# Loading the last quarter row of six tiles in two parts, in a row-wise maximum that skips NaN

## The chip, the cores and the metric

The kernel runs on one core of one Trainium2 chip. The metric is device time in microseconds (us) of one execution; lower is better.

## The reference

```python
def setup_inputs():
    batch, seq, dim = 32, 2048, 2048
    x = np.random.randn(batch, seq, dim).astype(np.float32)
    mask = np.random.rand(batch, seq, dim) < 0.1
    x[mask] = np.nan
    return {"x": x, "axis": -1}

def reference(x, axis):
    return np.nanmax(x, axis=axis).astype(np.float32)
```

For each of 65536 rows of 2048 floats it takes the largest value that isn't NaN. That is 537 MB to read and 0.26 MB to write.

## The kernel before

The rows are split into groups, and within a group each of the 128 partitions holds a run of whole rows that lie behind each other in memory. The work goes through tiles. A tile is one entry of `TILES`: a triple of loads, cleaning pieces and reductions, each counted in quarter rows of 512 floats (`Q`), that is 2 KB in each partition. The first tile has 4 quarter rows, nearly all others have 28, seven whole rows in every partition (7168 KB in all); the tiles of the last stage have 28 too, but are loaded in two to nine parts. Three buffers `xt` take the tiles in turn.

A tile goes through four steps, on four queues:

- **SP** issues its loads at line 309 (SP is the sync engine's queue, and the sixteen DMA engines carry the loads out). A load waits until DVE has done the last reduction of the tile that held the buffer before (`free`), and until the load that used the same semaphore before has landed (`lanes`; there are 14 semaphores, taken in turn). SP works strictly in order.
- **ACT** reads the upper 16 bits of each float and makes an ordered key of them in a buffer `kt` (line 227); a key piece waits for the loads that overlap its columns.
- **POOL** writes keys back to the upper halves in `xt` in such a way that NaN becomes very small (line 237); some pieces go to ACT instead.
- **DVE** takes the maximum over each row into `acc` (line 244).

In a usual tile the pieces are 7, 9 and 12 quarter rows and the reductions 16 and 12. The class `Order` (`add`, line 220) keeps the order by semaphores: each engine has one that counts its instructions, each load semaphore counts 16 a load, and an instruction waits only for what its engine has not already seen. At the end, six stores bring the maxima out.

What the change touches is the loop over a tile's loads:

```python
                for c in loads:
                    c *= Q
                    a, b = at, at + c
                    e = order.add("sp", nc.sync,
                        lambda: nc.sync.dma_start(
                            out=xt[:, a:b], in_=xg[:, base + a : base + b]),
                        before + lanes[turn], lane=f"load{turn}", step=16)
```

Of the kernel before, what the change touches and what calls it, by code (L numbers as in the profile page):

```python
# [10 lines left out]
Q = D // 4  # L11
# [43 lines left out]

APART = (70, 71, 72, 73)
WIDE = 7
BUFS = 3

KEYS = 3 * D  # L60
# [18 lines left out]
def total(pieces):  # L79
    return sum(sum(map(abs, p)) if isinstance(p, tuple) else abs(p) for p in pieces)  # L80
# [93 lines left out]
def kernel(  # L174
# [16 lines left out]
    P = nc.NUM_PARTITIONS  # L191
# [21 lines left out]
    top, warm = scalars[:, 0:1], scalars[:, 1:2]  # L213
    xts = [sing.tile([P, WIDE * D], i32, name=f"xt{i}") for i in range(BUFS)]
    kts = [sing.tile([P, KEYS], u16, name=f"kt{i}") for i in range(NKEYS)]
# [4 lines left out]
    with tc.tile_critical():  # L220
# [51 lines left out]

        free = [[] for _ in range(BUFS)]
        kfree = [[] for _ in range(NKEYS)]
# [8 lines left out]
        number = 0  # L283
# [6 lines left out]
        for gi, (s, g) in enumerate(zip(rows, GROUPS)):  # L290
            xg = xr[r0 : r0 + P * s].rearrange("(p s) d -> p (s d)", p=P)
# [4 lines left out]
            base = 0  # L296
            for loads, pieces, reds in g:
                assert sum(loads) == total(pieces) == sum(reds)
                xt, before = xts[number % BUFS], free[number % BUFS]
                number += 1  # L300
                landed = []
                at = 0
                for c in loads:
                    c *= Q
                    a, b = at, at + c
                    e = order.add(
                        "sp",
                        nc.sync,
                        lambda: nc.sync.dma_start(  # L309
                            out=xt[:, a:b], in_=xg[:, base + a : base + b]  # L310
                        ),
                        before + lanes[turn],
                        lane=f"load{turn}",
                        step=16,
                    )
                    lanes[turn] = [e]
                    turn = (turn + 1) % LANES
                    landed.append((a, b, e))
                    at += c
                clean = []  # L320
                after = []
                at = done = 0
# [41 lines left out]
                for parts in pieces:  # L364
                    parts = parts if isinstance(parts, tuple) else (parts,)
                    c = int(sum(map(abs, parts))) * Q
                    here = [l for a, b, l in landed if a < at + c and b > at]
                    kold = []
                    if used + c > KEYS:
# [9 lines left out]
                        out=kts[key][:, used : used + c],  # L379
                        in_=xt[:, at : at + c].bitcast(i16)[:, 1::2],  # L380
# [6 lines left out]
                    for c in parts:  # L387
                        back, wait, c = c < 0, isinstance(c, float), int(abs(c)) * Q
# [8 lines left out]
                        else:  # L397
# [3 lines left out]
                                out=to,  # L401
# [9 lines left out]
                        while reds and done + reds[0] <= min([at] + open_):  # L411
# [8 lines left out]
                            else:  # L420
# [5 lines left out]
                                out=to,  # L426
                                in_=xt[:, lo:done]
# [6 lines left out]
                            after.append(e)  # L434
                free[(number - 1) % BUFS] = after[-1:]
                base += at
# [65 lines left out]
```

## Time and profile before

| | before |
|---|---|
| time, median of 2 runs | 1251.94 us (1251.53 to 1252.36) |
| time of the profiled execution | 1251.85 us |
| its span in the profile | 1250.1 us |
| busy: POOL, DVE, ACT | 1168.7, 1110.8, 965.5 us |
| DMA, mean over the span | 430 GB/s |

The span runs from the first to the last instruction of the program; the 1.75 us beside it lie around it. In the profile an engine's busy time leaves out its waits. A DMA engine moves packets; here a packet is what a load brings to one partition, and a small packet of 4 bytes behind a load's last one raises the load's semaphore by one. The load has landed when the semaphore has come to 16 more. Line 309 names the issue of a load, 227 the keys, 237 POOL's pieces and 244 the reductions.

### The profile page before, as it was taken

The page shows a single profiled execution, that of the slowest core. Times are in us where ns is not written, and L with a number is a line of the kernel's source. Part 1 is how long each engine was busy: PE and PEld are TensorE (multiplying, and loading weights), DVE is VectorE, ACT ScalarE, POOL GpSimd, SP SyncE. Part 2 cuts the span into 40 slices and gives each one's busy share as a digit, 9 for nine tenths or more (in the row PEclk, how much of TensorE's full clock was granted, in tenths as well). Part 3 has the DMA queues.
Part 4 walks back from the last instruction along what each step waited for, and adds up shares of the span by engine and source line. Part 5 has one row for each costly group of instructions (what it writes and reads, how often), then busy time and mean ns, then how long its engine had stood idle before and what let it go on. Part 6 is the DMA issues. An engine that isn't in the chain of part 4 may idle for free.

```text
span 1250.1 us, 886 instructions
## 1 busy us (share of the span) xinstructions
DVE 1110.8 (89%) x181; ACT 965.5 (77%) x273; POOL 1168.7 (93%) x242
## 2 busy tenths in 40 slices
DVE  0788989888889888898988888988888999999999
ACT  3777887778777877788777877777777778999998
POOL 2999989998999899998999899999999999989998
DMA  9999999999999999999999999999999999999997
GB/s 415 435 417 440 440 440 429 422 441 440 435 420 437 440 437 433 422 440 440 437 429 426 440 440 433 422 437 440 437 433 422 441 437 423 438 431 429 428 428 311
DMA packets 15991, 537.20 MB, mean 430 GB/s; under 512 B 2544, under 2 KB 2544, under 8 KB 3568
## 3 DMA queue, kind: packets, MB, share of 16 engines
q1 hardware_dynamic: 15984, 537.14, 99.4%
q14 instruction: 7, 0.06, 0.0%
HBM read 536.87 MB, written 0.26 MB: 430 GB/s over the span
## 4 chain that ended last, share of the span: by engine, by line
DMA 40%; DVE 29%; POOL 22%; ACT 9%; issue 1%; SPq 0%
DMA xt<-in_x_dram 40%; DVE acc L244 29%; POOL xt L237 22%; ACT kt L227 8%; ACT xt L227 1%; SPq L309 0%; DVE none L250 0%; DVE acc L264 0%; SPq L465 0%; SPq L220 0%
## 5 line engine op out<-in xcount | busy, mean ns | idle before, releaser
L237 POOL TENSOR_SCALAR xt<-kt 128x3584 int16<-128x3584 uint16 (+11 forms) x236 | 1167.6, 4948 | 77.6 <-ACT kt L227 63.5
L244 DVE TENSOR_REDUCE acc<-xt 128x3 f32<-128x6144 f32 (+4 forms) x175 | 1107.5, 6379 | 136.6 <-POOL xt L237 129.2
L227 ACT ACTIVATE kt<-xt 128x3584 uint16<-128x3584 int16 (+9 forms) x247 | 913.4, 3734 | 278.3 <-DMA xt<-in_x_dram 258.1
L227 ACT ACTIVATE xt<-kt 128x512 int16<-128x512 uint16 (+6 forms) x24 | 52.9, 2203 | 0.7
L227 ACT ACT_TABLE_LOAD x1 | 1.3, 1283 | 0.9 <-SPq L220 0.9
L244 DVE TENSOR_REDUCE xt<-xt 128x1 f32<-128x1536 f32 x1 | 1.7, 1742 | 0.0
L270 DVE MEMSET scalars<- 128x1 f32 x1 | 0.1, 59 | 1.0 <-SPq L220 1.0
L250 DVE TENSOR_SCALAR none<-acc 128x414 int32<-128x414 f32 (+1 forms) x2 | 0.8, 380 | 0.1
L264 DVE TENSOR_TENSOR acc<-acc,none 128x414 int32<-128x414 int32 (+1 forms) x2 | 0.7, 374 | 0.1
L250 POOL TENSOR_SCALAR late<-acc 128x91 int32<-128x91 f32 x1 | 0.5, 547 | 0.1
L264 POOL TENSOR_TENSOR acc<-acc,late 128x91 int32<-128x91 int32 x1 | 0.3, 341 | 0.1
L483 POOL MEMSET const-float32-0.0<- 128x1 f32 x1 | 0.1, 99 | 0.2 <-issue 0.2
L227 ACT ACTIVATE scalars<-scalars 128x1 f32<-128x1 f32 x1 | 0.2, 203 | 0.0
L483 POOL MEMSET const-bfloat16-1.0<- 128x1 bf16 x1 | 0.1, 102 | 0.0
L483 POOL MEMSET const-uint8-127<- 128x1 uint8 x1 | 0.1, 102 | 0.0
L483 POOL MEMSET const-float32-1.0<- 128x1 f32 x1 | 0.1, 99 | 0.0
## 6 DMA issues: line engine op xcount, KB each, us to landing
xt<-in_x_dram SPq DMA_DIRECT2D x61, 7168.0 KB, 22.6
xt<-in_x_dram SPq DMA_DIRECT2D x2, 5120.0 KB, 17.5
xt<-in_x_dram SPq DMA_DIRECT2D x3, 2816.0 KB, 22.7
xt<-in_x_dram SPq DMA_DIRECT2D x4, 2048.0 KB, 22.3
xt<-in_x_dram SPq DMA_DIRECT2D x5, 1536.0 KB, 29.1
xt<-in_x_dram SPq DMA_DIRECT2D x2, 3584.0 KB, 24.7
xt<-in_x_dram SPq DMA_DIRECT2D x6, 1024.0 KB, 26.8
xt<-in_x_dram SPq DMA_DIRECT2D x3, 1792.0 KB, 30.0
```

The costliest lines, as they stand in the source:

```text
L227: lambda: nc.scalar.activation(**kw),
L237: lambda: nc.gpsimd.tensor_scalar(**kw),
L244: return order.add("dve", nc.vector, lambda: do(**kw), deps)
L250: lambda: engine.tensor_scalar(out=none, in0=acc, scalar1=NONE, scalar2=float(0x00800000), op0=ALU.is_equal, op1=ALU.mult,),
L264: lambda: engine.tensor_tensor(out=bits, in0=bits, in1=none, op=op),
L270: e_top = order.add("dve", nc.vector, lambda: nc.vector.memset(top, EDGE), [])
L483: nc = _bacc.Bacc("TRN2", target_bir_lowering=False, num_devices=1)
```

## The change

In the tiles with `number` 4 to 9 (`number` counts from 1) the single load of 28 quarter rows becomes three: 27 quarter rows of all 128 partitions, then the last quarter row of the first 120, 126, 117, 108, 121 or 100 partitions, then the last quarter row of the other 8, 2, 11, 20, 7 or 28. SP issues them in this order. Each has a semaphore of its own from the 14. `landed` gets the column range of each, and so the key pieces that overlap the last quarter row wait for three loads.

```diff
+CUTS = {4: 120, 5: 126, 6: 117, 7: 108, 8: 121, 9: 100}
...
-                for c in loads:
-                    c *= Q
-                    a, b = at, at + c
+                cut = CUTS.get(number)
+                runs = [(sum(loads[: i + 1]) * Q, 0, P) for i in range(len(loads))]
+                if cut:
+                    (end, _, _), *rest = runs
+                    runs = [(end - Q, 0, P), (end, 0, cut), (end, cut, P), *rest]
+                for b, p, q in runs:
+                    a = at
                     e = order.add(
                         "sp",
                         nc.sync,
                         lambda: nc.sync.dma_start(
-                            out=xt[:, a:b], in_=xg[:, base + a : base + b]
+                            out=xt[p:q, a:b], in_=xg[p:q, base + a : base + b]
                         ),
...
-                    at += c
+                    if q == P:
+                        at = b
```

Nothing else is changed: the other tiles' loads, the key pieces, the cleaning and the reductions stand as before. The loads become 12 more.

## The prediction

> **What bounds the kernel now.** First the page's rows on the DMA engines, with the row of the loads' sizes:
>
> ```profile
> DMA  9999999999999999999999999999999999999997
> q1 hardware_dynamic: 15984, 537.14, 99.4%
> xt<-in_x_dram SPq DMA_DIRECT2D x61, 7168.0 KB, 22.6
> ```
>
> The 16 DMA engines are busy for 99.4% of the span, in every slice but the last. Then the windows by stage, for the long middle (columns: stretch, its length, busy time of DVE, ACT and POOL, clock, DMA share, GB/s):
>
> ```profile
> 210.00:850.00 640.00, 572.42 (x77) 488.40 (x118) 609.93 (x111) 1.00 1.00 434
> ```
>
> POOL works 609.93 of 640 us, which is near, but the DMA share is 1.00. Next the waits, of the engines and of SP's queue:
>
> ```profile
> ACT kt L227 <- DMA xt<-in_x_dram: 258.1, 69, 15.0
> ```
>
> ```profile
> SPq L309 <- DVE acc L244: 1155.7, 71, 37.8
> ```
>
> ACT, the first engine to touch a tile, waits for a landing at nearly every tile. SP waits for DVE to give a buffer back, which looks as if DVE set the pace. The chain in order of time says whether it does:
>
> ```profile
> 67.83 22.62 DMA xt<-in_x_dram
> 90.45 0.02 issue
> 90.47 3.20 ACT kt L227
> ...
> 103.38 15.16 DVE acc L244 x2
> 118.54 0.02 issue
> 118.56 22.67 DMA xt<-in_x_dram
> ```
>
> DVE frees the buffer at 67.8 and the load that it releases lands at 90.45; the load before it landed at 73.58 (last increment of its semaphore). So the load is issued 5.8 us before the transfer ahead of it ends, and queues. The chain's "DMA 40%" is mostly queueing, and the pace is the transfer itself: 16.9 us a tile. DVE and POOL have those 5.8 us to spare.
>
> The records of single packets say how fast a DMA engine is. A 57344-byte packet (one partition's 28 quarter rows) takes 2116 ns and the next starts 3 ns before it ends, 2113 ns a step; eight such packets and a 4-byte one of 6 ns make 16.91 us, the pace above. From the 10th to the 90th percentile the 2116 ns doesn't move, so no engine is slower than another. A packet of 2048 bytes, in the kernel's only 256 KB load, takes 84 ns, a step of 81. The two steps differ by 2032 ns over 54 KiB, 37.6 ns a KiB, which leaves some 6 ns for the packet itself; a packet of 55296 bytes is therefore 75.3 ns shorter than one of 57344.
>
> The sixteen increments of a load's semaphore say how the engines stand to each other. The first tile's come within 0.56 us, those at 560 us within 0.92, the last loads' within 1.3 to 1.4. The steps between fall at 246, 255, 386, 940, 999 and 1130 us, where the trace has 8 KB instruction packets (309 ns each) on one engine or another. At the end the engines stand, in us behind the last: 1.29, 1.25, 1.24, 1.24, 1.18, 1.17, 1.17, 1.07, 0.99, 0.90, 0.83, 0.80, 0.74, 0.40, 0.15, 0. The mean is 0.9. **The time is set by the DMA engine that ends last**, and all that better balance could give is these 0.9 us.
>
> **The change, part by part.** (1) In six tiles the 57344-byte packets become 55296: every engine has 48 of them, so it saves 48 x 75.3 ns = 3.61 us. (2) The 128 packets of 2 KB that this takes out come back in two loads a tile, 768 packets of 81 ns in all. Equally spread that is 48 an engine, 3.89 us. (3) Each of the 12 added loads ends with a 4-byte packet on each engine that it uses, at most 12 x 6 ns = 0.07 us. With an equal spread the sum is 3.89 - 3.61 + 0.07 = **+0.35 us**, the lower bound.
>
> (4) The spread can't be equal. The trace shows loads of 128 partitions alone, and in each every engine gets eight packets. No row shows 120 or 8 partitions. Bounds: the equal spread, +0.35 us, and all packets of a split load on one engine, 768 x 0.081 - 3.61 = +58.6 us. I take the case nearest to what is seen, equal shares for those engines that a load uses, on as many engines as divide its partitions, and the same ones left out each time: 15, 14, 13, 12, 11 and 10 engines for the large parts, with 8, 9, 9, 9, 11 and 10 packets each; 8, 2, 11, 10, 7 and 14 engines for the rests, with 1, 1, 1, 2, 1 and 2. Against 48, the sixteen engines then have +16, +16, five times +15, +14, +13, +13, +1, -11, -20, -29, -40 and -48 packets (they sum to 0). Each of the ten loaded engines ends later by 61 to 64 x 0.081 - 3.61 + about 0.07 = +1.4 to +1.64 us; the last is relieved by 3.61. Which of them are the late ones now the trace doesn't tell. If the last one is loaded (10 in 16), the end moves by +1.4 to +1.64. If it is relieved, the next counts: -0.15 + 1.6 = +1.45 at most; and if the five latest were all among the relieved, the others still make -0.8 + 1.4 = +0.6. Over all such orders I take **+1.4 us**. That an engine ends 3.6 us early buys nothing, since ACT needs all shares of a tile.
>
> [...]
>
> (5) SP issues 12 more loads of 0.33 to 0.43 us (the first three issues are 0.43 apart). SP is idle 1155.7 us, and the large part is issued first, as early as now; the small ones follow 0.8 us later, 22 us before they land. Cost nothing; without that cover 12 x 0.43 = 5.2 us. Behind them on SP stands the next tile's load, 16.9 us later. (6) The 14 load semaphores are taken in turn, so 12 more loads only rotate them; a load waits for the one 14 loads earlier, five tiles back in tiles 4 to 9. Nothing. (7) ACT's last key piece of these tiles now also waits for the two small loads. They land within some 1.5 us after the large part, and ACT comes to this piece 7.5 us after its first (39.73 and 47.23 in the timeline); behind it on ACT stands the next tile's first piece, which waits for its own load. Nothing; if a part came 10 us late, POOL's and DVE's 5.8 us would be used up first. (8) In the tail the engines follow the landings: ACT still waits 2.9 us for loads from 1195 us on, in six waits, so a later landing moves the end in full.
>
> The profiled execution took 1251.85 us (span 1250.1), 0.1 below the median of 1251.94. Sum: 1251.85 + 1.4 = **1253.3 us**, to a tenth; its own range is 1252.3 to 1254.
>
> **The rivals.** *Almost equal spread*: shares differ by at most one packet, and the loaded engines alternate. +0.35 us and a little, 1252.2. For it: 128 partitions spread evenly in every DMA; against: it needs unequal shares within a load, which none shows. *Two engines meet*: a partition of the split loads is written by another engine than in the loads of 128, and if neighbours then share a way into memory, packets take twice their time. Bound: all 64 small packets of an engine doubled, 64 x 0.081 = 5.2 us more, 1258.5; half of them, 1255.9. For it: the engines run at one unvarying rate, as if each had a way of its own; against: no row, since the trace has loads of 128 partitions alone. [...] *A gain*: the rows happen to be taken from the late engines alone. At best the mean of 0.9 less 0.35, -0.55 us, 1251.3; against it stand the +61 packets on ten engines. *Slower, by crowding*: the number of engines has to be a power of two that divides the partitions; 128 on 16 doesn't exclude it. Then 120, 126, 117, 108, 121 and 100 run on 8, 2, 1, 4, 1 and 4 engines, the rests on 8, 2, 1, 4, 1 and 4, and the first engine gets 368 + 32 = 400 packets: 400 x 0.081 - 3.61 + 0.07 = +28.9 us, 1280.8. It would be slower by over 2% (25 us) from 353 packets on one engine. No row speaks for it, and none excludes it. *No effect*: the extra is lost in the spread of runs, 1251.9.
>
> **How the numbers follow.** Forecast 0.65, almost equal 0.14, engines meeting 0.12, a gain 0.04, crowding 0.03, no effect 0.02. The range takes in the forecast, the almost equal spread and the meeting up to somewhat over its half: 1251.7 to 1256.5. About what a measurement of this kernel can tell from no change is 2%, 25 us: only crowding is slower by more than that, with a little for costs I don't see, 0.04; a gain of 25 us has no place in engines that are never idle, 0.01; within 2%, 0.95.
>
> **What would show it.** In the profile after: 12 more issues at the load's line, packets of 55296 bytes for tiles 4 to 9 and 768 more of 2048 bytes, 84 ns each (168 if engines meet). The increments of a small load's semaphore should be bunched by engines used, and the spread between first and last increment should grow from 0.5 us to 4 to 6 us between tiles 4 and 10, and stay there. The last load should land near 1244.0 instead of 1242.6. POOL, DVE and ACT keep their busy times to 1 us. I'd be wrong if a pause appears in the DMA rows after tile 4, if the spread stays near 1.3 us, if the tiles' pace leaves 16.9 us after tile 9, or if the end moves by more than 5 us.

## The result, and the profile after

The changed kernel takes 1259.61 us (1259.36 and 1259.86) against 1251.94: a ratio of 1.0063, 95% interval 1.0047 to 1.0079. In five later executions three gave 1256.89, 1260.71 and 1261.66 us, against 1251.97 (1.0055, 1.0035 to 1.0075). The comparisons leave out executions over 1.5% above a kernel's fastest; the other two of these five, at 1392 and 1445 us, are such, and the experiments show that the change itself makes them. The forecast was 1253.3 us, with a range up to 1256.5: its sign was right, its size too small.

The page after, rows on the DMA engines and the loads:

```profile
GB/s 413 433 414 378 418 436 425 425 438 438 432 436 434 432 434 428 438 438 434 436 432 432 438 427 436 438 438 432 432 434 436 428 431 431 430 431 432 430 427 309
DMA packets 16886, 537.20 MB, mean 427 GB/s; under 512 B 2671, under 2 KB 2671, under 8 KB 4463
q1 hardware_dynamic: 16879, 537.14, 99.4%
...
xt<-in_x_dram SPq DMA_DIRECT2D x55, 7168.0 KB, 22.6
xt<-in_x_dram SPq DMA_DIRECT2D x6, 6912.0 KB, 26.0
```

The engines are as busy as before, 99.4%, in a longer span (1258.1 us): they don't wait more, they take longer for the same bytes. The fourth slice of 31.5 us has 378 GB/s. The windows narrow it down:

```profile
40.00:107.00 67.00, 59.31 (x9) 49.42 (x12) 65.05 (x13) 1.00 1.00 423
107.00:130.00 23.00, 20.53 (x3) 12.90 (x4) 20.53 (x4) 1.00 1.03 357
...
150.00:850.00 700.00, 624.39 (x84) 535.95 (x131) 662.36 (x119) 1.00 1.00 434
```

The same stretch in the kernel before:

```profile
107.00:130.00 23.00, 21.22 (x4) 18.11 (x5) 22.44 (x5) 1.00 0.99 429
```

From 150 us on it is the 434 GB/s of before. While tile 8 is loaded it is 357, where the kernel before has 429. Waits and chain say the same from the other side:

```profile
ACT kt L229 <- DMA xt<-in_x_dram: 265.4, 70, 15.0
```

```profile
136.68 29.17 DMA xt<-in_x_dram
165.85 0.02 issue
165.87 3.20 ACT kt L229
...
193.95 22.56 DMA xt<-in_x_dram
```

ACT waits 7.3 us more for landings. The load issued at 136.68 (tile 10's) takes 29.17 us, one issued at 193.95 again 22.56. Busy times of the engines stay: DVE 1110.9, ACT 965.9, POOL 1169.0.

The last increments of each tile's loads, in us after those of before, and what each tile adds, beside what the prediction's shares give for the busiest engine (8 to 11 packets and the rest's, times 0.081, less 0.60):

| tile, first part | late by | added | by shares |
|---|---|---|---|
| 4, 120 | 0.45 | 0.56 | 0.14 |
| 5, 126 | 0.95 | 0.50 | 0.22 |
| 6, 117 | 1.64 | 0.69 | 0.22 |
| 7, 108 | 2.46 | 0.82 | 0.30 |
| 8, 121 | 6.81 | 4.35 | 0.38 |
| 9, 100 | 7.84 | 1.03 | 0.38 |
| 10, whole | 7.75 | -0.09 | 0 |

(Tiles 1 to 3, before any cut, stand at -0.11.)

The packet records show two things. First, where the small packets stand, at the joint between one tile's load and the next, many of them are stretched (451 of 768 take over 90 ns, the longest 187 and not 84), and so are the large ones beside them: most take 250 to 720 ns more than their usual 2041 or 2116, the longest 988. Second, behind tile 7's joint the stretch doesn't end: seven large packets of every engine, 112 in all, take 2454 to 2464 ns. This is a *slow step*: the time from one packet to the next is 1.206 times the usual, on all engines alike. It ends when tile 8's own small packets come. Seven packets of +0.42 us are 2.9 us.

### The profile page after: what moved, and what is told of

Its sections match the earlier page's. It is cut to its first block, busy times and chain, and to the rows that moved or that the text cites. A ratio compares the mean times of both kernels' runs of the same rounds, so it can differ in the third digit from the quotient of the medians.

```text
span 1258.1 us, 904 instructions
## 1 busy us (share of the span) xinstructions
DVE 1110.9 (88%) x181; ACT 965.9 (77%) x273; POOL 1169.0 (93%) x242
## 2 busy tenths in 40 slices
DMA packets 16886, 537.20 MB, mean 427 GB/s; under 512 B 2671, under 2 KB 2671, under 8 KB 4463
## 3 DMA queue, kind: packets, MB, share of 16 engines
q1 hardware_dynamic: 16879, 537.14, 99.4%
## 4 chain that ended last, share of the span: by engine, by line
DMA 38%; DVE 31%; POOL 22%; ACT 8%; issue 1%; SPq 0%
DMA xt<-in_x_dram 38%; DVE acc L246 31%; POOL xt L239 22%; ACT kt L229 7%; ACT xt L229 1%; SPq L315 0%; DVE none L252 0%; DVE acc L266 0%; SPq L472 0%; SPq L222 0%
```

## The experiments

Two theories on the loss beside the small packets: *crossing*, a partition of a part load is written by another engine than usual, and two engines meet on one way to it; and *shares*, engines with unequal work, or packets and loads as such. On the slow step: it follows from how the engines' traffic stands to each other, or it belongs to tile 8's own cut and addresses. All kernels change one line or two; where nothing else is said only `CUTS` (and a part of 128 gives no rest).

**Small packets without parts.** `CUTS = {n: 128 for n in range(4, 10)}`

> Tiles 4 to 9 load the last quarter row apart, but for all 128 partitions in one load: the same 2 KB packets and six added loads, equal shares, each partition with its usual engine. If the loss comes from packets, loads and waits as such, some +5 us or more stay. If it comes from parts of the partitions (unequal shares, engines that meet, and the slow stretch in tile 8), only the packets' own cost is left: 48 x 5.7 ns + 6 x 6 ns = +0.3 us, every packet of 55296 bytes at 2041 ns and every one of 2048 bytes at 84 ns.

1252.17 us against 1251.87, ratio 1.0002 (0.9993 to 1.0012), from 1252.11 to 1252.34 in ten executions, where the kernel before has 1251.70 to 1252.04. The stretch of the cuts, in the kernel before and in this one:

```profile
40.00:142.00 102.00, 91.35 (x13) 75.17 (x19) 99.92 (x19) 1.00 1.00 432
40.00:142.00 102.00, 91.76 (x13) 75.58 (x19) 100.29 (x19) 1.00 1.00 432
```

Every 2 KB packet takes 84 ns, and the stretch of the cuts runs at 432 GB/s in both. Packets, loads, SP's issues and ACT's added waits together cost the 0.3 us that were worked out. The loss comes from the parts.

**Tiles 4 to 7 alone.** `CUTS = {4: 120, 5: 126, 6: 117, 7: 108}`

> Only tiles 4 to 7 are split (120, 126, 117, 108). Theory A, standing: the engines' standing to each other after tile 7's parts makes the slow stretch, in which every packet took 2460 ns and not 2041. Then tile 8's whole load is slow too (57344-byte packets near 2116 x 1.205 = 2550 ns), and it goes on until something moves the engines against each other, so the time ends above +6 us and perhaps far above. Theory B, tile 8's own: the 121 split or its addresses make it. Then no packet after tile 7's parts is slow and the time is +2.5 us (the last landing of tile 7 was 2.46 us late).

1255.20 us, +3.3. No slow step in this execution; beside the small packets the stretch is there in each tile. That is neither reading's number: there is no slow tile 8, as theory B has it, but the loss is somewhat more than its 2.5 us.

**The same cuts ten tiles later.** `CUTS = {14: 120, 15: 126, 16: 117, 17: 108, 18: 121, 19: 100}`

> The same six splits in tiles 14 to 19. Theory A (standing): again a slow stretch at the fifth split tile, number 18, if the standing before is alike, total near +7.7 us. Theory B (tile 8's addresses): no slow stretch, total near +7.7 - 3.4 = +4.3 us. A slow stretch at another place would speak for the standing too.

1399.08 us. After tile 19's small packets, with whole loads alone, each 57344-byte packet takes 2551 ns, up to 1144 us:

```profile
320.00:1140.00 820.00, 611.43 (x81) 513.11 (x125) 652.32 (x119) 1.00 1.00 360
1150.00:1300.00 150.00, 144.66 (x27) 133.05 (x41) 138.01 (x30) 1.00 0.99 428
```

Neither reading's number, but the step belongs to no tile, nor to tile 8's addresses. At 1144.3 us the trace has an 8 KB instruction packet on one engine; packets that end after it get shorter, and by 1145.4 the step is 2116 again. Four instruction packets before it, two of them within the slow stretch, ended nothing.

**Tile 8 alone, twice.** `CUTS = {8: 121}`

> Only tile 8 is split, at 121. Theory A (standing): its large part runs at 2041 ns a packet, since no engine is ahead yet, and only the meeting at the parts is left, +0.5 to +1 us. Theory B (tile 8's own split or addresses): packets of 2460 ns in tile 8, +3.9 us or more.

1387.39 us: tile 8's large part at 2041 ns, as theory A had it, but from its small packets on every packet 2375 ns, 1.122 times, to the end.

```profile
130.00:1100.00 970.00, 774.72 (x103) 655.05 (x159) 823.82 (x149) 1.00 1.00 387
```

> The split of tile 8 alone (121 and 7 partitions) once more; the first look took 1387 us, with packets of 2375 ns and not 2116 from tile 9 to the end. If the kernel alone decides, all runs are near 1387 us. If chance decides, some are near 1253 us.

Nine executions between 1252.58 and 1253.02 us, one at 1387.22. It is chance in each execution. The nine give the loss without a slow step: 1.0007 (0.9997 to 1.0017), +0.86 us, of which the shares make 0.38. The interval takes in no change at all, yet all nine lie above the thirteen executions of the kernel before (at most 1252.19).

```profile
130.00:1100.00 970.00, 873.62 (x121) 744.63 (x183) 926.56 (x169) 1.00 1.00 434
```

The same kernel, the same windows, 434 GB/s in the one execution and 387 in the other.

**The changed kernel again.**

> The changed kernel once more. If the slow stretch of tile 8 follows from the kernel alone, the time is 1259 to 1260 us in all runs and tile 8's packets take 2460 ns again. If it is a matter of chance in each execution, the times scatter, some near 1256 us (no slow stretch), some far above 1260 us.

1445.24, 1256.89, 1260.71, 1392.12 and 1261.66 us: chance. The execution of 1445 us was profiled:

```profile
150.00:1200.00 1050.00, 783.21 (x104) 662.86 (x161) 829.47 (x151) 1.00 1.00 361
```

Its tile 5 and tile 8 were slow too; so different cut tiles began a slow step, and a later cut ended what an earlier one began. The last step, of some 2551 ns a packet from 150 us on, ended at 1225.4 us, again where an 8 KB instruction packet stands; packets that start from 1226.3 on take 2116 to 2122. Five such packets before it, within the step, ended nothing. In the profile after, tile 8's small packets ended the slow step after seven packets. The fastest execution, 1256.89 us, costs 4.9 us; no trace of it was kept.

**Equal shares, twice.** `CUTS = {n: 112 for n in range(4, 10)}`

> The last quarter row of tiles 4 to 9 in parts of 112 and 16 partitions: 16 divides both, so all engines get 7 and 1 packets, equal shares. If unequal shares are what hurts, only +0.35 us is left and no packet is longer than usual. If it is that a partition is written by another engine than in the loads of 128, the small packets and the large ones beside them are stretched here too, +0.3 to +0.6 us a tile, and a slow state can follow.

1389.31 us, with 2375 ns a packet after tile 9.

```profile
150.00:1100.00 950.00, 758.23 (x101) 642.13 (x156) 807.49 (x146) 1.00 1.00 387
```

> 112 and 16 partitions in tiles 4 to 9 once more (equal shares on 16 engines). In an execution without a slow step what is left is the engines' meeting beside the small packets: +2 to +3.5 us if it is that, +0.35 us if unequal shares make the loss. Slow steps in some of the executions if crossing starts them, in none if unequal shares do.

1395.50, 1393.15, 1393.48 and 1254.26 us against 1251.58. Equal shares fell into the slow step in four of five executions, and the one quiet one cost 2.7 us, where packets and loads make 0.35. In the profiled one, of 1395.50 us, tile 4's parts began the step, and the parts of the next five tiles did not end it. Unequal shares are not needed for either loss.

**Steps in one execution.** `CUTS = {8: 121, 14: 128, 20: 121, 26: 112, 32: 64, 38: 121}`

> Tile 8 at 121, then other cuts far apart, each a step in the trace: tile 14 with all 128 partitions in one small load, tile 20 at 121, tile 26 at 112, tile 32 at 64, tile 38 at 121. If the slow state hangs on how the engines stand to each other, cuts in parts of the partitions (20, 26, 32, 38) enter it, leave it or change its rate, and the cut of all partitions (14) does nothing. If it hangs on the first cut or its addresses, the rate stays as tile 8 left it.

1282.89 us. Tile 8's parts began a step of 2375 ns; tile 14's load of all partitions left it as it was; tile 20's parts ended it; the rest left none.

```profile
128.00:350.00 222.00, 176.72 (x25) 153.61 (x37) 185.25 (x34) 1.00 1.00 387
360.00:1100.00 740.00, 658.88 (x91) 557.89 (x137) 707.31 (x128) 1.00 1.00 431
```

**Halves of the partitions, no small packets.**

```diff
-CUTS = {4: 120, 5: 126, 6: 117, 7: 108, 8: 121, 9: 100}
+CUTS = {8: 64}
...
-                    runs = [(end - Q, 0, P), (end, 0, cut), (end, cut, P), *rest]
+                    runs = [(end, 0, cut), (end, cut, P), *rest]
```

> Tile 8 is loaded in two loads of 28 quarter rows, of partitions 0 to 63 and of 64 to 127; four packets of 57344 bytes on every engine in each, equal shares, and no small packets at all. If neighbouring partitions share a way into memory, half the partitions have half the ways, and two engines meet on each: packets of some 4.2 us and not 2.1 through the whole tile, 16.9 us more, near 1269 us (and a slow step may follow). If a packet's time hangs on its engine alone, 2116 ns and +0.01 us. [...]

1270.05 us against 1251.58, +18.5.

```profile
107.00:142.00 35.00, 26.52 (x4) 12.45 (x3) 19.85 (x4) 1.00 0.96 206
```

Most packets of tile 8 take 4490 ns, 2.12 times, on all engines, and one packet behind it they take 2116 again. Two engines on one way would make twice 2116, 4232; why it is 6% more isn't known. The bytes of a packet are the same, and so is the number on each engine (16 small packets more than before, 2560 for 2544 under 512 B: each half was on all 16 engines). So what a packet cost here, 4490 ns or 2116, hung on which partitions were loaded at the time. Over the two halves in turn the stretch has 206 GB/s; the same one in the kernel before has 423:

```profile
107.00:142.00 35.00, 31.43 (x5) 25.64 (x7) 34.28 (x7) 1.00 0.98 423
```

**Even and odd partitions.**

```diff
-CUTS = {4: 120, 5: 126, 6: 117, 7: 108, 8: 121, 9: 100}
+CUTS = {n: 2 for n in range(4, 10)}
...
-                    runs = [(end - Q, 0, P), (end, 0, cut), (end, cut, P), *rest]
+                    # even partitions, then odd ones
+                    runs = [(end - Q, 0, P), (end, 0, -2), (end, 1, P), *rest]
+                def rows_of(p, q):
+                    return slice(p, P, 2 if q < 0 or p else 1)
...
-                            out=xt[p:q, a:b], in_=xg[p:q, base + a : base + b]
+                            out=xt[rows_of(p, q), a:b], in_=xg[rows_of(p, q), base + a : base + b]
```

> The last quarter row of tiles 4 to 9 in two loads, of the even and of the odd partitions (64 each, four packets on every engine, equal shares). If an engine gets a run of the load's partitions in order, engine i now writes four of the eight partitions that it has in a load of 128, none meets another, and +0.35 us is all: no packet is longer, no slow step in any execution. If parts of the partitions hurt as such, or engines get partitions in another order, packets of 2048 bytes are stretched as in the other cuts (up to 187 ns), some +3 us, and slow steps come.

(In `CUTS` only the tiles count here, not the 2.) 1251.88 us against 1251.58, 1.0002 (0.9993 to 1.0011), ten executions between 1251.75 and 1252.33.

```profile
40.00:142.00 102.00, 91.71 (x13) 75.53 (x19) 100.26 (x19) 1.00 1.00 432
```

Two part loads a tile, of 64 partitions like the halves, and each 2 KB packet takes 84 ns: parts as such cost no more than the 0.3 us of packets and loads. What makes the loss is which partitions a part takes: runs of neighbours cost here (2.7 us in six tiles at 112 and 16, 18.5 in the halves of one), every second one didn't (0.3 us in six tiles). That is what crossing says. Which engine writes which partition the trace doesn't show, so that engines meet is the reading that fits all runs, the halves above all; and as every partition has its own region of the input, no run tells whether they would meet where the data are read or where they are written.

**A pause behind the cuts.** 112 and 16 partitions as above, and before the loads of certain tiles SP waits for the tile just before:

```diff
+                if number in (16, 24):
+                    before = before + free[(number - 2) % BUFS]
```

> 112 and 16 partitions in tiles 4 to 9, which left a slow step of 2375 ns to the end in four of five executions; besides, the loads of tiles 16 and 24 wait until DVE has done the tile just before, so that the DMA engines run dry for some 25 us at each. If the slow step is a matter of how the engines' traffic stands to each other, the pause ends it: packets of 2116 ns from tile 16 on, and a time near 1252 + 2 x 25 + 10 x 2.1 + 3 = 1325 us. If it is a state that an engine or the memory keeps, the packets stay at 2375 ns after the pauses, and the time is near 1430 us. If this execution doesn't fall into the slow step, it says nothing and takes about 1305 us.

1315.49 us, no slow step after tile 9: inconclusive (about 1305 us was expected for that case). Then with three series of cuts, and pauses at tiles 14, 30 and 46:

> Three series of six tiles cut at 112 and 16 partitions (tiles 4 to 9, 20 to 25, 36 to 41), and after each, at tiles 14, 30 and 46, a pause of the DMA engines of some 25 us, in which SP waits until DVE has done the tile before. At least one series should leave a slow step. If it hangs on how the engines' traffic stands to each other, packets are back at 2116 ns behind each pause; if an engine or the memory keeps it, the step goes on past the pauses until the next cut.

1368.96 us. The first series left a step of 2375 ns.

```profile
146.00:219.00 73.00, 56.81 (x9) 52.41 (x13) 58.98 (x11) 1.00 1.01 390
222.00:248.00 26.00, 22.20 (x4) 11.47 (x3) 16.57 (x4) 1.00 0.00 0
252.00:340.00 88.00, 53.03 (x8) 57.29 (x15) 62.17 (x12) 1.00 1.01 436
```

All packets of 57344 bytes before the pause take 259 ns more than 2116. Behind it the first of each engine takes 2114 to 3141 ns, a slow start as at the kernel's beginning (there 445 to 1274 ns for 8192 bytes, which later take 309), and then they are back at 2116 to 2189.

> The same kernel in a second execution, since which series leave a slow step is a matter of chance: the same two readings, more cases.

1363.08 us; its three series left no step that reached a pause, so it adds no case. One case, then: the step didn't outlast 26 us without loads. The case isn't clean, as an 8 KB instruction packet stands at the start of this pause too, at 222.0 us; but of 29 such packets that fell into a lasting slow step in the other traces, 27 ended nothing. All this speaks for the traffic's standing and against a state kept in an engine; it doesn't show it.

## Why the prediction was wrong

Parts (1) to (3), packets and loads, were right: +0.3 us with six added loads of all partitions, and +0.3 us with the twelve of even and odd ones. So were (5) to (8): SP's waits for DVE went from 1155.7 to 1156.5 us, the pace behind tile 9 is 16.89 us again (165.85 to 182.74), and the end moved with the landings: the last came 7.8 us later (1250.42 for 1242.63) and the profiled execution took 8.0 us more.

Of part (4) the shares were right. No row of before shows a load of fewer than 128 partitions, so they were an assumption; the trace after shows them. Where a part lands, its semaphore has 15 and 8 increments in tile 4, then 14 and 2, 13 and 11, 12 and 10, 11 and 7, 10 and 14: in each of the twelve loads the largest number up to 16 that divides its partitions (one more increment of each comes earlier, near its issue). The packets agree: 16886 in all, 895 more, are 768 of 2 KB and 127 small ones, and 127 is 15 + 14 + 13 + 12 + 11 + 10 for the large parts and 8 + 2 + 11 + 10 + 7 + 14 for the rests. So the engine counts of the forecast hold; that the same engines are left out each time shows in their spread alone. The step that failed is the price in the same part: 0.081 us for every small packet, whichever engine carries it, and nothing for the large packets beside it. That price was taken from a load of all 128 partitions, whose packets took 84 ns each. The sum of +1.4 us became +7.8 at the last landing: 1.6 by the shares of the busiest engine, as the prediction works them out, 2.9 in tile 8's slow step, and the remaining 3.3 us in stretched packets at the six joints. Without the slow step that leaves 4.9 us, the loss of the fastest execution (1256.89 us). The rival *two engines meet*, with a chance of 0.12, had the mechanism that the runs support, and its bound was too small: it doubled the small packets alone, 5.2 us, and took half for the range, where the large packets of other engines beside them are stretched as well, and where a slow step followed (2.9 us) that no row of before gives a price for.

The engines' spread was forecast at 4 to 6 us behind tile 10; it was 3.8, since the engines that run ahead lose more at the joints (at tile 4's, +606 ns on the large packet that starts first, +158 on the last). It didn't stay there either: 2.7 at 437 us, 1.8 at 1012. *Crowding* on a power of two is excluded by the 127, *almost equal spread* too. Not every load in parts was dear: the two halves cost 18.5 us, while the even and the odd partitions neither gained nor cost more than 0.3 us.

## What to carry to other kernels

In this load-bound kernel, whose DMA engines are busy for 99.4% of the span, a load of part of the partitions was not priced by its bytes: a 57344-byte packet took 2116 ns in a load of all partitions and 4490 in one of a half. What counted was which partitions it took; that an engine then meets others at its partitions fits the runs and is not shown. In a kernel like it, cut such loads along the columns, or try every second partition: both cost 0.3 us here, where with runs of neighbouring partitions a packet took up to 2.12 times as long. And time such a change over many executions: the two of the result agreed within 0.5 us, and two of the next five were over 130 us longer.

## What the runs showed of the hardware that was not expected

- After part loads all 16 engines fell, in some executions, into a common slow step, 1.122 or 1.206 times the usual (2375 or 2551 ns for 57344 bytes, 387 or 360 GB/s in all), and stayed there for hundreds of microseconds of whole loads. In every kept trace it began at a part load. One that lasted came in 2 of 11 executions with one cut tile, in 4 of 5 with 112 and 16 partitions in tiles 4 to 9 (with the series of the three pause runs, behind 5 of 12), and in none of the 20 with columns or with even and odd partitions.
- It ended at some later part loads, at two of the 29 8 KB instruction packets that fell into one, and once in a pause of 26 us. What in the traffic holds it was not found, and which cut will start it can't be told beforehand from the trace.
- All engines are alike: of the 7808 packets of 57344 bytes in the trace before, 7742 lie within 5 ns of 2116, and a slower engine alone would have 488.
